# Batched 64x64 matmul: three of the eight a tiles loaded in 8 KB rows by two casting transfers each, with no fp32 quarter

## The chip, the core and the metric

The kernel runs on one core of a Trainium2 chip. That core has five engines with instruction streams of their own: TensorE (PE; its weight loads are shown as PEld), VectorE (DVE), ScalarE (ACT), GpSimd (POOL) and SyncE (SP), and 16 DMA engines that move data between HBM and the on-chip SBUF. Three of the instruction streams issue transfers here, each into a queue of its own: SP into queue q1, ScalarE into q10, GpSimd into q0. Only GpSimd's transfers can convert the data type on the way. The metric is the device time of one execution in microseconds (us).

## What is computed

```python
a: float32 (1024, 64, 64)     b: float32 (1024, 64, 64)
out = np.matmul(a, b)         # 1024 products of 64 x 64 matrices, float32
```

Each input has 16.78 MB, and so has the output. The kernel multiplies in bfloat16 (bf16) and accumulates in fp32.

## The kernel before

**Tiles.** a comes in 8 tiles of 128 batches (`s` = 0 to 7, 2.1 MB each), b and the output in 16 tiles of 64 batches (`t` = 0 to 15, 1.05 MB each). The loop runs over t; tile s of a serves t = 2s and 2s + 1.

**Loading a.** `load_a(s)` cuts a tile into four quarters h (batch = 4g + h). Partition p of a quarter holds 16 consecutive rows of one matrix, 1024 fp32 numbers, 4 KB that are contiguous in HBM. Quarters 0 to 2 are loaded by GpSimd (line 74), which casts to bf16 on the way (`a_sb`); quarter 3 is loaded as fp32 by SP (line 78, `a_raw`) and cast by an engine. Both come from `a_pool` with three buffers each. Tile 0 is loaded in another way (`load_first_a`: four fp32 quarters, two on SP and two on ScalarE). Tiles 1 and 2 are asked for before the loop, 3 and 4 behind tile 1's transposes, tile s + 4 in the iteration t = 2s for s = 1 to 3.

**Loading b.** `load_b(t)` loads a whole tile in one transfer (rows of 512 B, line 97), on SP for even t and on ScalarE for odd t, from three buffers: b(t+3) is issued when b(t) was cast to bf16 (`cast`, line 173, VectorE but for t = 0 and part of 15). Each issuing engine works in order: what is behind a transfer that waits for its buffer waits too.

**Transposing a.** TensorE needs a with k on the partitions. Pairs of bf16 are handled as one fp32 element (bitcast). For tiles 0 and 4 to 7, `regroup` puts the quarters side by side, TensorE transposes them (line 138) and ScalarE copies the result out of PSUM (line 141). For tiles 1, 2 and 3 (`ON_DVE`), VectorE transposes in blocks of 32x32, once for each quarter (line 128), straight from the loaded tile; the fp32 quarter is first cast by ScalarE (line 126) into a buffer of `work`.

**Spreading.** `spread(t)` copies the transposed a into a block-diagonal tile `at_bd` (two buffers, zeroed once): four copies of 32 partitions for the TensorE tiles (line 164), eight for the VectorE tiles (line 154). Then `multiply(t)` runs 64 pairs of weight load and matmul (line 218), ScalarE copies the products out of PSUM (line 206, for late tiles with VectorE), and `store` writes them one iteration later: tiles 0 to 13 by GpSimd (line 195), 14 by SP, 15 by SP and ScalarE.

**Order.** The schedule is written by hand: each engine executes its instructions in the order of the Python program. On VectorE, from t = 0 on: spread(1), cast(1), the four transposes of tile 1, spread(2), cast(2), the four transposes of tile 2, spread(3), cast(3), two transposes of tile 3, spread(4), cast(4), the other two, spread(5), cast(5), and so on. On SP the order is half of tile 0, b0, a_raw of tile 1, b2, a_raw of tiles 2, 3 and 4, b4, a_raw of 5, b6 and so on; on GpSimd the casting loads of tiles 1, 2, 3 and 4, then the store of t = 0, tile 5, and stores and loads in turn.

Of the kernel before, what the change touches and what calls it, by code (L numbers as in the profile page):

```python
# [8 lines left out]
fp32 = mybir.dt.float32  # L9
bf16 = mybir.dt.bfloat16  # L10
# [3 lines left out]
def kernel(  # L14
# [14 lines left out]
    nc = tc.nc  # L29
# [9 lines left out]
    ON_DVE = (1, 2, 3)  # L39

    a_v = a.rearrange("(s g h) (mp v) k -> s h g mp (v k)", h=4, g=32, v=16)
    b_v = b.rearrange("(t g h) (kp u) n -> t (h kp) g (u n)", h=4, g=16, u=2)
    o_v = out.rearrange("(t gh x) (mo w) n -> t (x mo) gh (w n)", gh=8, x=8, w=4)

    consts = ctx.enter_context(tc.tile_pool(name="consts", bufs=1))
    a_pool = ctx.enter_context(tc.tile_pool(name="a_pool", bufs=A_AHEAD))
    b_pool = ctx.enter_context(tc.tile_pool(name="b_pool", bufs=B_AHEAD))
    work = ctx.enter_context(tc.tile_pool(name="work", bufs=2))
# [13 lines left out]
    a_tiles, b_tiles, abf_tiles, at_tiles, bbf_tiles = {}, {}, {}, {}, {}  # L62
# [5 lines left out]
        return nc.scalar if t == n_t - 1 and lo % 4 == 0 else nc.sync  # L68

    def load_a(s):  # L70

        a_sb = a_pool.tile([128, 3, 16, 64], bf16, name="a_sb")
        for h in range(3):
            nc.gpsimd.dma_start(  # L74
                out=a_sb[:, h, :, :].rearrange("p v k -> p (v k)"), in_=a_v[s, h], single_packet=True
            )
        a_raw = a_pool.tile([128, 16, 64], fp32, name="a_raw")
        nc.sync.dma_start(out=a_raw[:].rearrange("p v k -> p (v k)"), in_=a_v[s, 3])
        a_tiles[s] = a_sb, a_raw

    def load_first_a():

# [17 lines left out]
    def regroup(s):  # L100
        a_sb = a_tiles.pop(s)
        a_bf = work.tile([128, 16, 4, 64], bf16, name="a_bf")
        if s == 0:
            for h in range(4):
                copy = nc.scalar.copy if h % 2 else nc.vector.tensor_copy
                copy(a_bf[:, :, h, :], a_sb[h].rearrange("p (v k) -> p v k", v=16))  # L106
        else:
            cast_sb, raw = a_sb
            nc.vector.tensor_copy(  # L109
                a_bf[:, :, 0:3, :], cast_sb[:].rearrange("p h v k -> p v h k")  # L110
            )
            nc.vector.tensor_copy(a_bf[:, :, 3, :], raw[:])  # L112
        abf_tiles[s] = a_bf
        at_tiles[s] = work.tile([128, 32, 4, 4, 4], fp32, name="at_sb")

    def transpose_dve(s, half):
        cast_sb, raw = a_tiles[s]
        if half == 0:
            at_tiles[s] = work.tile([128, 4, 8, 4, 4, 4], fp32, name="at_sb")
        for h in (2 * half, 2 * half + 1):  # L120
            rows = cast_sb[:, h, :, :] if h < 3 else None
            if h == 3:
                rows = work.tile([128, 16, 4, 64], bf16, name="a_bf")[:, 0:4, :, :].rearrange(
                    "p x y k -> p (x y) k"
                )
                nc.scalar.copy(rows, raw[:])  # L126
            pairs = rows.rearrange("p v k -> p (v k)").bitcast(fp32)
            nc.vector.transpose(  # L128
                at_tiles[s][:, h].rearrange("p g w mp vo -> p w vo g mp"),
                pairs.rearrange("p (vo w kp) -> p w vo kp", vo=4, w=4),  # L130
            )

    def transpose(s, j):
        a_cols = abf_tiles[s][:].rearrange("p v h k -> p v (h k)").bitcast(fp32)
# [11 lines left out]
    def spread(t):  # L146
        bd = bd_tiles[t % N_BD]
        at_sb = at_tiles[t // 2]
        for h in range(4):
            rows = slice(32 * h, 32 * h + 32)  # L150
            if t // 2 in ON_DVE:
                for i in range(2):
                    block = 32 * (2 * (t % 2) + i)
                    nc.vector.tensor_copy(  # L154
                        bd[rows, 8 * i : 8 * i + 8, :, h, :, :].rearrange(
                            "p g w mp vo -> p (g w) (mp vo)"
                        ),
                        at_sb[block : block + 32, h].rearrange(
                            "p g w mp vo -> p (g w) (mp vo)"
                        ),  # L160
                    )
            else:
                half = slice(16 * (t % 2), 16 * (t % 2) + 16)
                nc.vector.tensor_copy(  # L164
                    bd[rows, :, :, h, :, :].rearrange("p g w mp vo -> p (g w) (mp vo)"),
                    at_sb[rows, half].rearrange("p g w mp vo -> p (g w) (mp vo)"),
                )
# [71 lines left out]
    with tc.manual_schedule():  # L239
# [7 lines left out]
        make_identity(nc, identity)  # L247
        nc.gpsimd.memset(bd_tiles[1][:, 0:8], 0.0)
        load_a(1)
        load_b(2)  # L250
        nc.gpsimd.memset(bd_tiles[1][:, 8:16], 0.0)
        load_a(2)
        regroup(0)
        transpose(0, 0)
        transpose(0, 1)
        spread(0)
        cast(0)
        for t in range(n_t):
            s, half = t // 2, t % 2
            if t + 1 < n_t:  # L260
                spread(t + 1)
                cast(t + 1)
            if t + B_AHEAD < n_t:
                load_b(t + B_AHEAD)
            if half == 0 and 0 < s < n_s - 1 - A_AHEAD:
                load_a(s + 1 + A_AHEAD)
            if half == 0 and 0 < s < n_s - 1 and s + 1 not in ON_DVE:
                transpose(s + 1, 1)
            multiply(t)
            if t == 0:  # L270
                transpose_dve(1, 0)
                transpose_dve(1, 1)
                a_tiles.pop(1)
                load_a(A_AHEAD)
                load_a(A_AHEAD + 1)
            if t and s + 2 in ON_DVE and (half or s):
                for part in [0, 1] if t == 1 else [half]:
                    transpose_dve(s + 2, part)
                if half:
                    a_tiles.pop(s + 2)  # L280
            elif half == 0 and 0 < s and s + 2 < n_s:
                regroup(s + 2)
            elif half == 1 and s + 2 < n_s:
                transpose(s + 2, 0)
            if t >= HOLD - 1:
                store(t - HOLD + 1)
# [32 lines left out]
```

## Time and profile before

| What | Value |
|---|---|
| Time, median of 3 runs | 133.86 us (133.62 to 133.91) |
| The profiled execution: its time, its span | 133.61 us, 131.8 us |
| Busy: DVE, ACT, PE, POOL | 101.8, 88.1, 59.6, 31.9 us |
| VectorE's transposes, line 128 | 9 of `a_sb`, mean 1065 ns; 3 of `a_bf`, mean 1049 ns |
| ScalarE's casts of the fp32 quarter, line 126 | 3, mean 1046 ns |
| Casting loads of a, line 74 | 21 of 256 KB written (half of what is read), median 15.9 us to landing |
| Plain loads of a quarter, line 78 | 7 of 512 KB, median 17.3 us to landing |
| Copies into the block diagonal, line 154 | 48 of 32x512, mean 457 ns |

The span runs from the first to the last instruction of the profiled execution; the time of an execution has some 1.8 us around it. The busy time of an engine says how long it had work, not that it set the pace: what counts is which wait ends last. A line of the timeline gives the start, the duration and the engine, the line of the kernel, the operation and its output and input, the number of instructions merged, and in brackets how long the engine had been idle and who ended that. In the windows each engine has its busy time and its number of instructions; then come TensorE's granted clock, the busy share of the DMA engines and the GB/s written. In the queue table a casting transfer counts with the bytes that it writes, half of those that it reads.

### The profile page before, as it was taken

The numbers are of one execution on the slowest core, as the hardware profiler recorded it, in microseconds if no ns is written. First come the engines' busy times: TensorE is split into PE (matmuls) and PEld (weight loads), VectorE is DVE, ScalarE is ACT, GpSimd is POOL, SyncE is SP. The second block draws the span as 40 slices with busy tenths as digits, with TensorE's granted clock in tenths as the row PEclk, the third lists the DMA queues.
The fourth block names the chain that finished last, engine by engine and source line by source line (L and its number), as shares of the span: only waits on it lengthen the run. The fifth ranks groups of instructions, "written<-read, shape, count | busy, mean of one in ns | idle before, by whom it ended". The sixth has DMA issues, their size and how long they took to land.

```text
span 131.8 us, 2750 instructions
## 1 busy us (share of the span) xinstructions
PE 59.6 (45%) x1104; PEld 56.7 (43%) x1104; DVE 101.8 (77%) x144; ACT 88.1 (67%) x158; POOL 31.9 (24%) x43
## 2 busy tenths in 40 slices
PE   0006405730550640908662883299369619465000
PEld 0006305730550630908552872298368618464000
DVE  5930399529999984999999998699999997898300
ACT  2125414999495096492999989469969996549920
POOL 8991000340054000618031204300420302040000
PEclk9999975798568555595999599558968975579855
DMA  3999999999999999999999999999999999999993
GB/s 68 372 334 313 306 313 280 280 311 321 327 299 400 362 306 297 393 393 400 321 285 357 403 395 362 308 299 385 395 391 393 390 390 397 399 395 406 390 383 136
DMA packets 19020, 44.99 MB, mean 341 GB/s; under 512 B 1088, under 2 KB 3136, under 8 KB 19008
## 3 DMA queue, kind: packets, MB, share of 16 engines
q0 software_dynamic: 6832, 20.19, 50.6%
q1 hardware_dynamic: 7120, 14.68, 30.7%
q10 hardware_dynamic: 5056, 9.96, 20.1%
q8 instruction: 8, 0.13, 0.4%
q14 instruction: 4, 0.03, 0.1%
HBM read 33.55 MB, written 16.78 MB: 382 GB/s over the span
## 4 chain that ended last, share of the span: by engine, by line
DMA 53%; ACT 15%; DVE 14%; PE 6%; issue 5%; SPq 2%; ACTq 0%; DVEq 0%
DMA b_sb<-in_b_dram 53%; ACT o_sb L206 12%; PE o_ps L218 6%; DVE at_bd L164 4%; DVE b_bf L173 4%; DVE at_bd L154 2%; ACT b_bf L173 1%; DVE at_sb L128 1%; DVE o_sb L206 1%; DVE a_bf L109 1%; SPq L91 1%; ACT a_bf L126 1%; SPq L97 1%; ACT b_bf L180 1%; DVE a_bf L112 0%
## 5 line engine op out<-in xcount | busy, mean ns | idle before, releaser
L206 ACT COPY o_sb<-o_ps 64x512 f32<-64x512 f32 x112 | 65.0, 581 | 17.9 <-PE o_ps L218 13.5
L218 PEld LDWEIGHTS <-at_bd 128*128 128x128 bf16 x1024 | 45.2, 117 | 52.6 <-DVE b_bf L173 40.5
L218 PE MATMUL o_ps<-b_bf,at_bd 128*128 128x64 bf16 x960 | 45.6, 223 | 48.7 <-DVE b_bf L173 35.0
L164 DVE COPY at_bd<-at_sb 32x1024 f32<-32x1024 f32 x40 | 29.6, 739 | 6.6 <-ACT at_sb L141 5.6
L195 POOL DMA_DIRECT2D out_dram<-o_sb x14 | 15.4, 1103 | 46.1 <-ACT at_sb L141 20.6
L154 DVE COPY at_bd<-at_sb 32x512 f32<-32x512 f32 x48 | 22.0, 457 | 1.1
L74 POOL DMA_DIRECT2D a_sb<-in_a_dram x21 | 12.4, 606 | 38.5 <-DVE at_sb L128 33.2
L173 DVE CAST b_bf<-b_sb 128x2048 bf16<-128x2048 f32 x14 | 17.2, 1227 | 5.2 <-DMA b_sb<-in_b_dram 4.9
L138 PE MATMUL at_ps<-identity,a_bf 128*128 128x128 f32 x80 | 12.9, 329 | 11.0 <-ACT a_bf L106 11.0
L138 PEld LDWEIGHTS at_ps<-identity,a_bf 128*128 128x128 f32 x80 | 11.7, 176 | 11.0 <-issue 11.0
L141 ACT COPY at_sb<-at_ps 128x512 f32<-128x512 f32 x20 | 10.8, 591 | 2.7 <-PE at_ps L138 2.0
L128 DVE STREAM_TRANSPOSE at_sb<-a_sb 128x512 f32<-128x512 f32 x9 | 8.9, 1065 | 0.0
L128 DVE STREAM_TRANSPOSE at_sb<-a_bf 128x512 f32<-128x512 f32 x3 | 3.1, 1049 | 4.0 <-ACT a_bf L126 4.0
L206 DVE COPY o_sb<-o_ps 64x512 f32<-64x512 f32 x8 | 5.5, 690 | 0.2
L106 ACT CAST a_bf<-o_sb 128x1024 bf16<-128x1024 f32 x2 | 2.1, 1045 | 5.0 <-DMA o_sb<-in_a_dram 5.0
L173 ACT CAST b_bf<-b_sb 128x2048 bf16<-128x2048 f32 x1 | 1.9, 1897 | 4.0 <-DMA b_sb<-in_b_dram 4.0
L126 ACT CAST a_bf<-a_raw 128x1024 bf16<-128x1024 f32 x3 | 3.1, 1046 | 1.7 <-DMA a_raw<-in_a_dram 1.7
L109 DVE COPY a_bf<-a_sb 128x3072 bf16<-128x3072 bf16 x4 | 4.2, 1045 | 0.0
L106 DVE CAST a_bf<-o_sb 128x1024 bf16<-128x1024 f32 x2 | 2.8, 1383 | 1.8 <-DMA o_sb<-in_a_dram 1.8
L246 DVE MEMSET at_bd<- 128x4096 f32 x1 | 3.5, 3472 | 0.8 <-issue 0.8
L206 DVE COPY o_sb<-at_ps 64x256 f32<-64x256 f32 x8 | 3.4, 422 | 0.5 <-PE at_ps L218 0.4
L180 ACT CAST b_bf<-b_sb 128x512 bf16<-128x512 f32 x2 | 1.1, 616 | 3.5 <-DMA b_sb<-in_b_dram 3.5
(16 smaller groups left out, 15.4 us busy)
## 6 DMA issues: line engine op xcount, KB each, us to landing
out_dram<-o_sb POOLq DMA_DIRECT2D x14, 1024.0 KB, 22.7
a_sb<-in_a_dram POOLq DMA_DIRECT2D x21, 256.0 KB, 15.9
a_raw<-in_a_dram SPq DMA_DIRECT2D x7, 512.0 KB, 17.3
o_sb<-in_a_dram SPq DMA_DIRECT2D x2, 512.0 KB, 5.9
o_sb<-in_a_dram ACTq DMA_DIRECT2D x2, 512.0 KB, 7.0
out_dram<-o_sb SPq DMA_DIRECT2D x2, 512.0 KB, 5.5
out_dram<-o_sb SPq DMA_DIRECT2D x2, 256.0 KB, 5.2
out_dram<-o_sb ACTq DMA_DIRECT2D x2, 256.0 KB, 4.7
```

The costliest lines, as they stand in the source:

```text
L74: nc.gpsimd.dma_start(out=a_sb[:, h, :, :].rearrange("p v k -> p (v k)"), in_=a_v[s, h], single_packet=True)
L106: copy(a_bf[:, :, h, :], a_sb[h].rearrange("p (v k) -> p v k", v=16))
L109: nc.vector.tensor_copy(a_bf[:, :, 0:3, :], cast_sb[:].rearrange("p h v k -> p v h k"))
L128: nc.vector.transpose(at_tiles[s][:, h].rearrange("p g w mp vo -> p w vo g mp"), pairs.rearrange("p (vo w kp) -> p w vo kp", vo=4, w=4),)
L138: nc.tensor.transpose(at_ps[:, vo, :], a_cols[:, 4 * vo + 2 * j + wl, :], identity[:])
L141: nc.scalar.copy(at_tiles[s][:, :, 2 * j + wl, :, :], at_ps[:].rearrange("p vo (g mp) -> p g mp vo", mp=4),)
L154: nc.vector.tensor_copy(bd[rows, 8 * i : 8 * i + 8, :, h, :, :].rearrange("p g w mp vo -> p (g w) (mp vo)"), at_sb[block : block + 32, h]. ...
L164: nc.vector.tensor_copy(bd[rows, :, :, h, :, :].rearrange("p g w mp vo -> p (g w) (mp vo)"), at_sb[rows, half].rearrange("p g w mp vo -> p ...
L173: (nc.vector.tensor_copy if t else nc.scalar.copy)(b_bf[:], b_sb[:])
L195: store_queue(t, lo).dma_start(out=o_v[t, :, lo : lo + n, :], in_=o_sb[:, lo : lo + n].rearrange("p gh j wl n -> p (gh j wl n)"),)
L206: copies[2 * par + wl](dst, src)
L218: nc.tensor.matmul(o_ps[:, gl, g % 2, j, :], at_bd[:, j, g, :, u], b_bf[:, g, 64 * u : 64 * u + 64], start=(u == 0), stop=(u == 1),)
```

## The change

Tiles 1 to 3 are cut into two halves instead of four quarters (batch = 2g + h; partition p holds 32 consecutive rows of one matrix, 2048 fp32 numbers, 8 KB contiguous in HBM). Each half is one casting transfer on GpSimd, and both halves have the same form: there is no fp32 quarter in these tiles, no transfer of one on SP and no cast of it on ScalarE. VectorE transposes a half in one instruction of 1024 fp32 elements for each partition. In the transposed tile, a row of a matrix is now found at (gm, vo) with 4 x 8 in place of (mp, vo) with 4 x 4, where gm holds the parity of g beside the half of the matrix; `spread` picks the 2 x 8 block that belongs to a copy, so that each of its runs is 16 elements of 64 bytes as before, with 128 bytes from one run to the next in the source instead of 64. The other tiles are loaded as before, but from one room for all kinds of tile: `a_sb` and `a_raw` are now parts of one buffer of 10,240 bytes per partition, the same size as the two had together.

In the order of each engine: SP no longer has the a_raw of tiles 1, 2 and 3, so that b2 follows b0, then come a_raw of tile 4, b4, a_raw of 5, b6. GpSimd issues two loads, not three, for each of tiles 1 to 3. VectorE has one transpose where it had two.

```diff
+    a_v8 = a.rearrange("(s g h) (mp v) k -> s h g mp (v k)", h=2, g=64, v=32)
...
     def load_a(s):
-        a_sb = a_pool.tile([128, 3, 16, 64], bf16, name="a_sb")
+        room = a_pool.tile([128, 5120], bf16, name="a_sb")
+        if s in ON_DVE:
+            a_sb = room[:, 0:4096].rearrange("p (h x) -> p h x", h=2)
+            for h in range(2):
+                nc.gpsimd.dma_start(out=a_sb[:, h, :], in_=a_v8[s, h], single_packet=True)
+            a_tiles[s] = a_sb
+            return
+        a_sb = room[:, 0:3072].rearrange("p (h x) -> p h x", h=3)
         for h in range(3):
-            nc.gpsimd.dma_start(
-                out=a_sb[:, h, :, :].rearrange("p v k -> p (v k)"), in_=a_v[s, h], single_packet=True
-            )
-        a_raw = a_pool.tile([128, 16, 64], fp32, name="a_raw")
-        nc.sync.dma_start(out=a_raw[:].rearrange("p v k -> p (v k)"), in_=a_v[s, 3])
-        a_tiles[s] = a_sb, a_raw
+            nc.gpsimd.dma_start(out=a_sb[:, h, :], in_=a_v[s, h], single_packet=True)
+        raw = room[:, 3072:5120].bitcast(fp32)
+        nc.sync.dma_start(out=raw, in_=a_v[s, 3])
+        a_tiles[s] = (
+            a_sb.rearrange("p h (v k) -> p h v k", v=16),
+            raw.rearrange("p (v k) -> p v k", v=16),
+        )
...
-    def transpose_dve(s, half):
-        cast_sb, raw = a_tiles[s]
-        if half == 0:
-            at_tiles[s] = work.tile([128, 4, 8, 4, 4, 4], fp32, name="at_sb")
-        for h in (2 * half, 2 * half + 1):
-            rows = cast_sb[:, h, :, :] if h < 3 else None
-            if h == 3:
-                rows = work.tile([128, 16, 4, 64], bf16, name="a_bf")[:, 0:4, :, :].rearrange(
-                    "p x y k -> p (x y) k"
-                )
-                nc.scalar.copy(rows, raw[:])
-            pairs = rows.rearrange("p v k -> p (v k)").bitcast(fp32)
-            nc.vector.transpose(
-                at_tiles[s][:, h].rearrange("p g w mp vo -> p w vo g mp"),
-                pairs.rearrange("p (vo w kp) -> p w vo kp", vo=4, w=4),
-            )
+    def transpose_dve(s, h):
+        if h == 0:
+            at_tiles[s] = work.tile([128, 2, 8, 4, 4, 8], fp32, name="at_sb")
+        nc.vector.transpose(
+            at_tiles[s][:, h].rearrange("p g w gm vo -> p w vo g gm"),
+            a_tiles[s][:, h, :].bitcast(fp32).rearrange(
+                "p (vo w kp) -> p w vo kp", vo=8, w=4
+            ),
+        )
...
             if t // 2 in ON_DVE:
+                gp = h // 2
...
-                        at_sb[block : block + 32, h].rearrange(
+                        at_sb[block : block + 32, h % 2, :, :, 2 * gp : 2 * gp + 2, :].rearrange(
```

More of the change, by code (lines that the diff above doesn't have):

```diff
@@ L109, in regroup @@
             nc.vector.tensor_copy(
-                a_bf[:, :, 0:3, :], cast_sb[:].rearrange("p h v k -> p v h k")
+                a_bf[:, :, 0:3, :], cast_sb.rearrange("p h v k -> p v h k")
             )
-            nc.vector.tensor_copy(a_bf[:, :, 3, :], raw[:])
+            nc.vector.tensor_copy(a_bf[:, :, 3, :], raw)
         abf_tiles[s] = a_bf
         at_tiles[s] = work.tile([128, 32, 4, 4, 4], fp32, name="at_sb")
-    def transpose_dve(s, half):
-        cast_sb, raw = a_tiles[s]
-        if half == 0:
-            at_tiles[s] = work.tile([128, 4, 8, 4, 4, 4], fp32, name="at_sb")
-        for h in (2 * half, 2 * half + 1):
-            rows = cast_sb[:, h, :, :] if h < 3 else None
-            if h == 3:
-                rows = work.tile([128, 16, 4, 64], bf16, name="a_bf")[:, 0:4, :, :].rearrange(
-                    "p x y k -> p (x y) k"
-                )
-                nc.scalar.copy(rows, raw[:])
-            pairs = rows.rearrange("p v k -> p (v k)").bitcast(fp32)
-            nc.vector.transpose(
-                at_tiles[s][:, h].rearrange("p g w mp vo -> p w vo g mp"),
-                pairs.rearrange("p (vo w kp) -> p w vo kp", vo=4, w=4),
-            )
+    def transpose_dve(s, h):
[7 more added lines that the diff above has]
+        )
     def transpose(s, j):
```

## The prediction

> **What bounds the kernel now.** First the page's slices, its HBM line and the queue table; then the chain that ended last; then the DMA queues cut to short windows; then VectorE's timeline.
>
> The page: busy tenths of the 16 DMA engines in 40 slices, GB/s moved in each, HBM bytes.
> ```profile
> DMA  3999999999999999999999999999999999999993
> ...
> HBM read 33.55 MB, written 16.78 MB: 382 GB/s over the span
> ```
> The transfers fill every slice but the two at the ends. 50.33 MB at 382 GB/s is the span, 131.8 us. What the change could save on an engine is therefore worth only what it does to the transfers, or to the tail after the last load.
>
> The chain that ended last (start us, us, what):
> ```profile
> 2.48 16.73 DMA b_sb<-in_b_dram
> ...
> 29.93 21.27 DMA b_sb<-in_b_dram
> ...
> 51.23 1.23 DVE b_bf L173
> ...
> 102.47 14.73 DMA b_sb<-in_b_dram
> ...
> 125.87 0.37 ACT o_sb L206
> ```
> The chain is made of waits for b loads, and behind the last one (b15, landing at 117.2) of ScalarE's evacuations until 126.2 and the last stores.
>
> The queue table of the window 10 to 18 us (packets, MB written, share): q0 is GpSimd's queue, q1 SP's, q10 ScalarE's.
> ```profile
> q0 software_dynamic: 416, 0.76, 49.9%
> q1 hardware_dynamic: 415, 0.85, 30.7%
> q10 hardware_dynamic: 417, 0.85, 27.4%
> ```
> Here q0 carries casting a rows (4 KB read, 2 KB written), q1 and q10 carry b in packets of 2 KB. The three queues take turns packet by packet, 416 : 415 : 417. In bytes read q0 therefore has a half and b0 and b1 a quarter each (0.85 MB in 8 us is 106 GB/s). Whoever has larger packets has more of the bandwidth: this carries the prediction.
>
> VectorE's timeline:
> ```profile
> 20.93 1.23 DVE L173 CAST b_bf<-b_sb 128x2048 bf16<-128x2048 f32 x1
> 22.07 2.87 DVE L128 STREAM_TRANSPOSE at_sb<-a_sb 128x512 f32<-128x512 f32 x3
> 28.93 1.06 DVE L128 STREAM_TRANSPOSE at_sb<-a_bf 128x512 f32<-128x512 f32 x1 [3.99 <-ACT a_bf L126]
> 29.84 3.44 DVE L154 COPY at_bd<-at_sb 32x512 f32<-32x512 f32 x8
> 33.30 1.23 DVE L173 CAST b_bf<-b_sb 128x2048 bf16<-128x2048 f32 x1
> ...
> 45.68 3.50 DVE L154 COPY at_bd<-at_sb 32x512 f32<-32x512 f32 x8
> 51.23 1.23 DVE L173 CAST b_bf<-b_sb 128x2048 bf16<-128x2048 f32 x1 [2.04 <-DMA b_sb<-in_b_dram]
> ```
> VectorE loses 3.99 us to ScalarE's cast of the fp32 quarter, then makes up the time and waits 2.04 us for b4 all the same.
>
> The tail, in windows (the last number is GB/s):
> ```profile
> 126.00:128.00 2.00, 0.00 (x0) 0.00 (x0) 0.00 (x0) 0.24 (x1) 0.00 (x0) 0.50 1.08 382
> 128.00:130.00 2.00, 0.00 (x0) 0.00 (x0) 0.00 (x0) 0.00 (x0) 0.00 (x0) 0.50 0.86 301
> 130.00:132.00 2.00, 0.00 (x0) 0.00 (x0) 0.00 (x0) 0.00 (x0) 0.00 (x0) 0.50 0.08 26
> ```
> From 126 us on 1.42 MB move (2 x 0.382 + 2 x 0.301 + 2 x 0.026), the last packet near 130.6. At the 401 GB/s of the window 116 to 120 (q0 alone) they need 3.54 us, not 4.6. So an earlier end of the evacuations can win at most 1.05 us; beyond that the bytes decide.
>
> **The change part by part.** All sums stand against the profiled execution's 133.61 us (span 131.8), which is 0.25 us under the median 133.86.
>
> *Transfers.* Bytes in HBM stay. For tiles 1 to 3, 1,152 cast packets of 4 KB and 384 plain ones of 4 KB become 768 of 8 KB (source sides). Packet records (medians): cast 172 ns, plain 4 KB 159 to 172, b's 2 KB 84. Two of 84 are 168, so a packet's fixed part lies between nothing and 9 ns: 768 x 9 / 16 engines = 0.43 us gained at most. If the fp32 quarters at 159 ns become cast bytes at 172: 384 x 13 / 16 = 0.31 us lost. Between these I take 0, as the plain quarter's median is 172 too.
>
> *Issue.* POOL issues 18 a transfers, not 21 (mean 606 ns, 1.8 us less); SP loses three issues, and ScalarE three casts of 1.05 us. None of these engines sets the end in that stage, so 0. On SP, b2 and b4 are no longer queued behind a_raw 1 to 3 (1.57 MB); a_raw of tile 4 now waits for the second transpose of tile 1, with b4 behind it.
>
> *VectorE.* Twelve transposes of 512 columns become six of 1024. Three took 2.87 us, 0.957 each; two of these are 1.91 us, less at most one fixed part (the 128x1 memset takes 59 ns): 1.85. Twice the longest single one, 1.085, is 2.17. I take 1.87, as pitch and not duration adds up. Wider target strides (32 B for 16) have no row. The 48 spread copies (L154, median 419 ns) now read 64-byte runs; their target already has such runs, so 0; the slow end is the PSUM copies' 690 ns for 512 columns, 13 us in all.
>
> *The start, by turns.* q0's first packet comes at 7.1 us. With 8 KB packets q0's share against 2 KB packets is 2/3, 268 of 402 GB/s, and b0 and b1 have 67 each.
> - The rest of a0 ends at 8.6 (q1) and 10.1 (q10), half a us to 1 us later; q0 has 0.65 MB by then and b0 0.09.
> - b0: 0.96 MB at 67 GB/s, 24.5 us (before: 18.9). b1: 1.05 MB, 25.8 (19.7).
> - a1 to a3, 6.29 MB: 4.84 by 25.8, then 4/5 of 402 beside b2 alone: 30.3 (32.9).
> - VectorE: cast(1) 26.2 to 27.4, two transposes to 31.1 (before 29.9), so spread(2) to 34.5; b2 lands near 32.5, so no wait: cast(2) 34.5, 1.2 us later than before.
> - a4 and b4 are issued at 31.1 (a4's casts before: 25.2). Until their first packet there is left 0.6 MB of b2 and b3's 1.05 MB (issued 26.8 behind ScalarE's cast): 1.65 MB, 4.1 us from 30.3, to 34.4. Issue to first packet took 1.4 us at the start (0.74 to 2.16) and 4.4 for b3 (21.2 to 25.6): 32.5 to 35.5. So the DMA engines stand idle for 0 to 1.1 us. I take 0.7, nearer the loaded case.
> - Then q1 has a_raw 4 alone ahead of b4: 0.52 MB at 200 GB/s and 1.05 at 133, later 100: b4 near 47 (50.8). VectorE gets there through cast(2) 34.5, transposes 39.5, spread(3) 43, cast(3) 44.2, transpose 46.1, spread(4): cast(4) at 49.6, 1.6 us earlier than 51.23.
> - ScalarE's issue of b7 waits for this cast (52.5, now 50.9), and from b7 on q10 goes on from load to load to b15. So b15 can land up to 1.6 us earlier.
>
> *Sum.* Tail: 1.6, capped by the bytes at 1.05 us gained. DMA idle near 32 us: 0.7 lost. Price of packets 0. Net -0.35: 133.26, with 0.25 to the median 133.5.
>
> Two rules of the Trainium skill speak against the change. "DMA: Bandwidth & Descriptors" (section SWDGE vs HWDGE vs iDMA) wants a packet of GpSimd's queue to be at most 4096 B; q0 shows none above that before, in 10 to 18 us 172 ns each. If the rows are cut to it, the shares stay as they are and the sum would be the -1.05 us of the second rival. "SBUF — State Buffer" (section SBUF: two separate sides) says that VectorE's two-port copies lock GpSimd out from writing descriptors, while SP's transfers are immune; the first cast's packet at 7.14, 4.1 us behind its issue at 3.00 and just as VectorE's cast of 2.07 us ended, agrees. By it a4 would begin behind spread(2)'s copies, at about 34.5 to 35.5, idle 1.1 us, and the sum would be +0.05: 133.9.
>
> **The rivals.**
> 1. *The DMA engines run dry (slower).* Place: 30 to 36 us, between a3's landing and a4's first packet. For it: b0, the start of all compute, lands 5.6 us later, and a4 is issued 5.9 us later. Against: b2 and b3 bridge 4.1 us. Price: 1.1 us of idle by the long latency, and no lead carried to the tail: 133.61 + 1.1 + 0.25 = 135.0. It decides from 1.05 us of idle on, that is if a4's first packet comes after 35.4; each us that the transposes take beyond 1.87 x 2 adds as much.
> 2. *The rows are cut into 4 KB packets.* Shares as before, b0 at 18.9; no 3.99 us wait, spread(2) at 25.8 and not 29.8, a4 not late, no idle. The tail's cap alone: -1.05, 132.8. For it: no larger packet is in the trace; against: a plain row of 4 KB is one packet, and so is a cast one.
> 3. *Hidden anyway.* b15's landing is set by q10's share beside the stores, and the lead only makes VectorE wait (as the 2.04 us did): 133.9.
> 4. *The spread copies lose their rate.* VectorE has some 2 us of slack until 51 us, so it begins at 2 / 48 = 42 ns each; at 690 ns it costs 11 us, 145. Against: the L164 copies, 739 ns for 1024 columns, have the same rate as L154.
>
> **How the numbers follow.** The runs before lie within 0.2% of their median, so 0.27 us is about what can be told from no change. Chances: forecast 0.38 (133.5, own range 132.9 to 134.0), rival 1 0.28, rival 2 0.14, rival 3 0.14, rival 4 0.06. Faster: 0.38 x 0.75 + 0.14 x 0.95 + 0.14 x 0.2 = 0.45. Slower: 0.28 x 0.9 + 0.06 x 0.95 + some 0.02 each of the forecast and rival 3 = 0.35. Same: 0.20. Range: below, 1.05 and 0.43 off the median, 132.4; above, rival 1 with 0.2 us of dearer packets or transposes, 135.2. Rival 4's far end and a little on either side stay outside.
>
> **What would show it.** Right: packets of 4096 B written on q0 before 31 us, twice as long as the 172 ns; q0 : q1 : q10 still equal in packets but b0's cast on ScalarE starting near 24.9, not 19.2; a short hole in the DMA slices near 31 to 35 us; VectorE's wait for b4 gone and its cast(4) before 51.2; the last evacuation before 126.2. Wrong: b0 at 19 (rival 2), transposes much over 1.9 us or copies L154 over 460 ns (rivals 1 and 4), a hole over 1 us (rival 1), b15 landing at 117 in spite of a lead (rival 3).

## The result, and the profile after

The changed kernel takes 135.31 us (median of 5, 135.08 to 135.44) against 133.86 us for the kernel before on the same chip (median of 5, 133.57 to 133.99). The ratio is 1.0113, with a 95% interval of 1.0098 to 1.0129: slower by 1.1%. The profiled execution took 135.31 us with a span of 133.5 us; the one of before took 133.61 us with 131.8 us. So 1.7 us have to be found.

The page of the changed kernel: busy tenths of the DMA engines, the groups of the spread copies and of VectorE's transposes (busy us, mean ns of one, idle before), HBM bytes.

```profile
DMA  3999999999999999999999999999999999999992
...
HBM read 33.55 MB, written 16.78 MB: 377 GB/s over the span
...
L156 DVE COPY at_bd<-at_sb 32x512 f32<-32x512 f32 x48 | 21.8, 454 | 1.1
...
L127 DVE STREAM_TRANSPOSE at_sb<-a_sb 128x1024 f32<-128x1024 f32 x6 | 11.5, 1966 | 0.0
```

The same bytes at 377 GB/s instead of 382. There is no hole in the DMA slices, none that would show in tenths. The transposes and the copies cost what was expected.

The queue table of the changed kernel from 10 to 18 us (packets, MB written, share):

```profile
q0 software_dynamic: 294, 1.07, 66.1%
q1 hardware_dynamic: 289, 0.59, 21.4%
q10 hardware_dynamic: 290, 0.58, 18.6%
```

The packets of the three queues are still equal in number, but q0's are now written in 4 KB (8 KB read). So b0 and b1 come later, as VectorE's timeline shows (start, duration, work, in brackets the wait before it):

```profile
25.18 1.23 DVE L175 CAST b_bf<-b_sb 128x2048 bf16<-128x2048 f32 x1 [3.35 <-DMA b_sb<-in_b_dram]
26.32 3.80 DVE L127 STREAM_TRANSPOSE at_sb<-a_sb 128x1024 f32<-128x1024 f32 x2
29.98 3.64 DVE L156 COPY at_bd<-at_sb 32x512 f32<-32x512 f32 x8
34.22 1.23 DVE L175 CAST b_bf<-b_sb 128x2048 bf16<-128x2048 f32 x1 [0.60 <-DMA b_sb<-in_b_dram]
...
50.13 1.23 DVE L175 CAST b_bf<-b_sb 128x2048 bf16<-128x2048 f32 x1
```

cast(1) is at 25.18 (before: 20.93), cast(4) at 50.13 without a wait (before: 51.23 with one of 2.04). The compute has overtaken the kernel before by 1.1 us there, and keeps that to the end. The chain that ended last (start us, us, what) shows it at b15:

```profile
3.67 30.46 DMA b_sb<-in_b_dram
34.22 1.23 DVE b_bf L175
...
100.68 15.04 DMA b_sb<-in_b_dram
```

The last long wait ends at 115.72, before at 117.20. Compute ended earlier, and the kernel still became slower. So the loss must be in the transfers. The queue tables from 30 to 36 us, of the kernel before and then of the changed one:

```profile
q1 hardware_dynamic: 259, 0.97, 42.6%
q0 software_dynamic: 256, 0.46, 40.7%
q10 hardware_dynamic: 259, 0.53, 23.2%
```

```profile
q10 hardware_dynamic: 527, 1.05, 61.8%
q1 hardware_dynamic: 291, 0.70, 35.9%
q0 software_dynamic: 45, 0.08, 7.2%
```

GpSimd's queue is all but empty in these 6 us, because a3 has landed (30.5 us, from the packet records) and a4 has only just been asked for. GpSimd's timeline shows the request, for which GpSimd had waited 21.71 us, until the transposes of tile 1 were done (before: at 25.23):

```profile
30.42 1.63 POOL L81 DMA_DIRECT2D a_sb<-in_a_dram  x3 [21.71 <-DVE at_sb L127]
```

But the engines are not idle. The windows of the changed kernel (busy us and number of instructions of PE, PEld, DVE, ACT, POOL; clock; DMA share; GB/s written):

```profile
30.00:32.00 2.00, 1.10 (x32) 1.00 (x32) 1.95 (x6) 1.95 (x4) 1.58 (x3) 1.00 1.04 327
32.00:34.00 2.00, 1.30 (x25) 1.30 (x25) 1.55 (x4) 1.94 (x5) 1.10 (x2) 0.62 1.06 291
34.00:36.00 2.00, 1.07 (x21) 0.91 (x19) 1.78 (x2) 1.95 (x5) 0.10 (x1) 0.50 1.08 304
```

A share of 1.04 to 1.08 says busy throughout, yet only 291 to 327 GB/s arrive, and what arrives here is nearly all plain, so that written is also read. Reckoned in bytes read, with q0's counted twice, the changed kernel has 1.05 + 0.70 + 0.16 = 1.91 MB in these 6 us, 318 GB/s, and the kernel before 0.97 + 0.92 + 0.53 = 2.42 MB, 403 GB/s. A packet of b3 takes 118 ns here (median); before, and beside larger packets, one of b takes 84 to 96.

**A ledger of the transfers.** To put prices on places, I added up the bytes read of all packets (casting packets by what they read) in stretches of the span, and took from each stretch's length what these bytes would need at 400 GB/s. The result is us lost against 400 GB/s; below zero, the stretch ran faster.

| Stretch, us | before | after | difference |
|---|---|---|---|
| 0 to 8 | 2.98 | 3.03 | +0.05 |
| 8 to 30 | -0.10 | -0.67 | -0.57 |
| 30 to 36 | -0.08 | 1.22 | +1.30 |
| 36 to 124 | 0.44 | 0.50 | +0.06 |
| 124 to the last landing | 1.08 | 1.45 | +0.37 |
| last landing | 130.58 | 131.76 | +1.18 |
| from there to the end of the span | 1.24 | 1.76 | +0.52 |

The stretches add up to 1.21 us (the last landing is 1.18 us later), and with the 0.52 us behind it they are the 1.7 us: 1.3 lost in the stretch 30 to 36 us, 0.57 won before it by the larger packets, 0.37 lost in the tail, and 0.5 behind the last landing. Most of the last is, by the records of the instructions, GpSimd's clearing of the semaphores at the end: it began 0.35 us behind TensorE's drain in the changed kernel (133.06 and 132.71 us) and together with it before (131.37 and 131.38).

The tail of the changed kernel in windows (columns as above):

```profile
124.00:126.00 2.00, 0.00 (x0) 0.00 (x0) 0.00 (x0) 0.73 (x2) 0.00 (x0) 0.66 1.03 370
126.00:128.00 2.00, 0.00 (x0) 0.00 (x0) 0.00 (x0) 0.00 (x0) 0.00 (x0) 0.50 1.05 359
128.00:130.00 2.00, 0.00 (x0) 0.00 (x0) 0.00 (x0) 0.00 (x0) 0.00 (x0) 0.50 1.04 348
130.00:132.00 2.00, 0.00 (x0) 0.00 (x0) 0.00 (x0) 0.00 (x0) 0.00 (x0) 0.50 0.50 172
```

ScalarE has finished by 125 us (before: 126.2), but 2.5 MB are still to be stored (2 x 370 + 2 x 359 + 2 x 348 + 2 x 172, in KB/us). GpSimd's stores, which came late with everything else in the queues, land at 126.9 (before: 125.2, both by packet records). What was won on the engines found the DMA engines still full.

### The profile page after: what moved, and what is told of

Same layout as the page of the kernel before. It is cut to its first block, busy times and chain, and to the rows that moved or that the text cites. A ratio compares the mean times of both kernels' runs of the same rounds, so it can differ in the third digit from the quotient of the medians.

```text
span 133.5 us, 2737 instructions
## 1 busy us (share of the span) xinstructions
PE 62.5 (47%) x1104; PEld 59.4 (44%) x1104; DVE 101.2 (76%) x138; ACT 84.9 (64%) x155; POOL 32.6 (24%) x40
## 4 chain that ended last, share of the span: by engine, by line
DMA 46%; DVE 28%; ACT 9%; issue 6%; SPq 2%; PE 1%; DVEq 0%; ACTq 0%
DMA b_sb<-in_b_dram 46%; ACT o_sb L208 9%; DVE at_bd L156 8%; DVE at_bd L166 6%; DVE at_sb L127 6%; DVE b_bf L175 5%; PE o_ps L220 1%; DVE a_bf L120 1%; SPq L105 1%; DVE o_sb L208 1%; SPq L99 1%; DVE a_bf L117 1%; ACT b_bf L182 1%; ACT at_sb L142 0%; DVEq L208 0%
## 5 line engine op out<-in xcount | busy, mean ns | idle before, releaser
L220 PEld LDWEIGHTS <-at_bd 128*128 128x128 bf16 x1024 | 47.4, 119 | 49.1 <-DVE b_bf L175 33.5
L220 PE MATMUL o_ps<-b_bf,at_bd 128*128 128x64 bf16 x960 | 46.4, 224 | 45.1 <-DVE b_bf L175 31.5
L197 POOL DMA_DIRECT2D out_dram<-o_sb x14 | 16.6, 1189 | 38.6 <-ACT at_sb L142 15.3
L139 PEld LDWEIGHTS at_ps<-identity,a_bf 128*128 128x128 f32 x80 | 12.2, 182 | 12.0 <-issue 12.0
L127 DVE STREAM_TRANSPOSE at_sb<-a_sb 128x1024 f32<-128x1024 f32 x6 | 11.5, 1966 | 0.0
L114 DVE CAST a_bf<-o_sb 128x1024 bf16<-128x1024 f32 x2 | 2.2, 1098 | 2.6 <-DMA o_sb<-in_a_dram 2.5
L220 PE MATMUL at_ps<-b_bf,at_bd 128*128 128x64 bf16 x64 | 3.6, 241 | 0.9 <-ACT b_bf L182 0.9
```

Source lines behind the costliest of these rows:

```text
L127: nc.vector.transpose(at_tiles[s][:, h].rearrange("p g w gm vo -> p w vo g gm"), a_tiles[s][:, h, :].bitcast(fp32).rearrange("p (vo w kp) ...
L139: nc.tensor.transpose(at_ps[:, vo, :], a_cols[:, 4 * vo + 2 * j + wl, :], identity[:])
L197: store_queue(t, lo).dma_start(out=o_v[t, :, lo : lo + n, :], in_=o_sb[:, lo : lo + n].rearrange("p gh j wl n -> p (gh j wl n)"),)
L220: nc.tensor.matmul(o_ps[:, gl, g % 2, j, :], at_bd[:, j, g, :, u], b_bf[:, g, 64 * u : 64 * u + 64], start=(u == 0), stop=(u == 1),)
```

## The experiments

Four theories were set against each other.

1. *The gap alone*: the stretch at 30 to 36 us costs the time, by the low rate of b's packets alone.
2. *The late start of compute*: b0 and b1 land 5 us later, and this is what costs.
3. *The burden on GpSimd's queue*: three more quarters go through casting transfers of GpSimd.
4. *Three places*, formed after the first runs: the gap, a stall at 8 to 12 us in some variants, and the tail, each costing what its rate says.

In the diffs, `s in (...)` lists the tiles that are loaded in rows of 8 KB; the others of tiles 1 to 3 get two transfers for each half, with rows of 4 KB. All ratios are to the kernel before on the same chip, with a 95% interval.

### Rows of 4 KB in all three tiles

```diff
             for h in range(2):
-                nc.gpsimd.dma_start(out=a_sb[:, h, :], in_=a_v8[s, h], single_packet=True)
+                runs = [slice(0, 2048)] if s in () else [slice(0, 1024), slice(1024, 2048)]
+                for r in runs:
+                    nc.gpsimd.dma_start(out=a_sb[:, h, r], in_=a_v8[s, h][:, :, r], single_packet=True)
```

> The changed kernel with one thing undone: each half of tiles 1 to 3 is loaded by two casting transfers of 4 KB rows, not by one of 8 KB rows. No fp32 quarter, the large transposes and the queues stay as changed. Theory 1 (the gap: 8 KB packets double GpSimd's share, b0 and b1 come 5 us late, a4 is asked for late, and between a3's landing and a4's first packet only b's packets are left, which move at 290 GB/s where 400 are usual): b0 lands near 19 us, no window of 30 to 36 us under 390 GB/s read, time 133.0 to 133.9. Theory 2 (late start: compute begins 5 us late and this is never made up): the same here, 133.0 to 133.9. Theory 3 (burden: three quarters more on GpSimd's queue push its stores back into the tail): stays at 135.3.

Measured: 134.96 against 133.58 us, 1.0104 (1.0089 to 1.0118). The gap at 30 to 36 us is gone (ledger -0.01 us), b0 is cast at 20.4 us (before: 19.2, changed: 24.1), and the kernel is nearly as slow as the changed one. Theories 1 and 2 missed the time. The ledger shows two other places: 0.54 us lost at 8 to 12 us, and 1.75 us behind 124 us. The first one in windows, of the kernel before and then of this one:

```profile
9.00:10.00 1.00, 0.00 (x0) 0.00 (x0) 0.66 (x1) 0.14 (x1) 0.78 (x1) 1.00 1.10 301
```

```profile
9.00:10.00 1.00, 0.00 (x0) 0.00 (x0) 0.69 (x1) 0.00 (x0) 1.00 (x2) 1.00 0.96 211
```

In this us the rate falls from 301 to 211 GB/s written with the engines 0.96 busy; a casting packet takes 222 ns there on average instead of 172, one of SP's b 118 instead of 96. The medians stay at 172 and 96, so it is some packets that take much longer. Theory 3 hit the time; the run with quarters below shows that its reason was wrong.

### 8 KB rows in tiles 1 and 2 only

```diff
-                runs = [slice(0, 2048)] if s in () else [slice(0, 1024), slice(1024, 2048)]
+                runs = [slice(0, 2048)] if s in (1, 2) else [slice(0, 1024), slice(1024, 2048)]
```

> 8 KB rows for tiles 1 and 2, 4 KB rows (two transfers for each half) for tile 3. b0 and b1 should still land near 24 and 25 us, but tile 3 lasts until about 33 us, so that the gap is filled. Theory 1 (gap): most of the loss is gone, 133.6 to 134.2. Theory 2 (late start): stays at 135.3. Theory 3 (burden): stays at 135.3.

Measured: 134.46 us, 1.0066 (1.0051 to 1.0081). b0 is as late as in the changed kernel (24 us), and tile 3 keeps GpSimd's queue going longer. Its queue table from 30 to 36 us:

```profile
q10 hardware_dynamic: 524, 1.04, 54.4%
q0 software_dynamic: 190, 0.35, 31.2%
q1 hardware_dynamic: 139, 0.43, 21.0%
```

With 190 packets of q0 in the place of 45, the stretch loses 0.54 us, not 1.22, and the ratio is 0.5% below the changed kernel's. As b0 is just as late, this speaks against theory 2, and as the load on GpSimd's queue is the same, against theory 3. Theory 1 missed too, by 0.3 us: the gap is only half filled, and 1.46 us are lost behind 124 us.

### 8 KB rows in tile 3 only

```diff
-                runs = [slice(0, 2048)] if s in () else [slice(0, 1024), slice(1024, 2048)]
+                runs = [slice(0, 2048)] if s in (3,) else [slice(0, 1024), slice(1024, 2048)]
```

> 8 KB rows for tile 3 alone, 4 KB rows for tiles 1 and 2. b0 lands near 19 us, and the 8 KB packets come when b0 and b1 have landed. Theories 1 and 2: no gap, no late start, 133.0 to 133.8. Theory 3 (burden): 135.3.

Measured: 134.96 us, 1.0099 (1.0081 to 1.0118). No gap (-0.14 us), but the stall at 8 to 12 us again (0.65 us) and 1.92 us behind 124. Theories 1 and 2 missed once more. What the runs with the stall share is tile 1 in rows of 4 KB, each of them one half of 8 KB.

### The rates by themselves

A kernel that leaves out the product and only moves data: each stage starts when the one before has landed. The lines are shortened.

```diff
+        for t in range(6):                       # A: b alone, SP and ScalarE
+            load_b(t)
+        nc.gpsimd.dma_start(out=a4[i][:, 1024 * h : 1024 * h + 1024], in_=a_v[i, h], single_packet=True)       # B
+        nc.gpsimd.dma_start(out=a8[i][:, 2048 * h : 2048 * h + 2048], in_=a_v8[2 + i, h], single_packet=True)  # C
...                                              # D: as C beside b; E: 4 KB rows, no cast; F, G: stores
```

> No matmul: the kernel only moves data, in stages that wait for one another, and leaves the product out. Stage A: six b tiles on SP's and ScalarE's queues alone. B: casts of 4 KB rows alone. C: casts of 8 KB rows alone. D: casts of 8 KB rows beside b. E: plain 4 KB rows on two queues. F: stores by GpSimd. G: stores by SP and ScalarE. Theory 1 (gap): A runs near 290 GB/s, B near 400, C near 410 to 420 (source bytes), D near 410, so that it is the lack of other packets beside b's that costs. Theories 2 and 3: A near 400 as everything else, and the low rate at 30 to 36 us was a lack of requests.

Measured, in windows inside the stages (busy DVE, ACT, POOL; clock; DMA share; GB/s written). In order: A b alone; B casts of 4 KB; C casts of 8 KB; D casts of 8 KB beside b, and in the row behind it the rest of b alone, when the casts have landed; E plain 4 KB rows; F stores of GpSimd; G stores of SP and ScalarE.

```profile
6.00:22.00 16.00, 2.32 (x32) 0.41 (x1) 0.00 (x0) 1.00 1.06 290
30.00:36.00 6.00, 1.78 (x20) 0.00 (x0) 0.22 (x1) 1.00 1.12 206
46.00:51.00 5.00, 1.16 (x16) 0.00 (x0) 0.00 (x0) 1.00 1.06 213
59.00:69.00 10.00, 0.95 (x12) 0.00 (x0) 0.00 (x0) 1.00 1.06 280
71.00:75.00 4.00, 0.94 (x12) 0.00 (x0) 0.00 (x0) 1.00 1.06 292
82.00:85.00 3.00, 0.67 (x8) 0.00 (x0) 0.00 (x0) 1.00 1.02 416
90.00:96.00 6.00, 0.15 (x1) 0.00 (x0) 0.93 (x2) 1.00 1.00 312
105.00:112.00 7.00, 0.00 (x0) 0.00 (x0) 0.00 (x0) 1.00 1.04 344
```

b alone moves 290 GB/s with the DMA engines 1.06 busy; the casts read 412 (4 KB) and 426 GB/s (8 KB), twice what they write; plain rows of 4 KB move 416, and the two mixed read some 414 (the casts' 1.34 MB written count twice, beside 0.73 MB in each of b's queues, in 10 us). When the casts are through, b falls to 292 at once. So the low rate of the gap is b's own rate when nothing larger runs beside it, without any compute: (2.4 - 6 x 0.290) / 0.4 = 1.65 us would be lost if the 6 us of the gap held b alone; with the few q0 packets and a_raw of tile 4 in it, 1.22 us were. The stores need care: F moves 312 GB/s here, where GpSimd's stores in the kernel before moved 401 (116 to 120 us), and why is open; so the 344 of G is a rate of this kernel and not a limit.

### 8 KB rows in tiles 1 and 3

```diff
-                runs = [slice(0, 2048)] if s in () else [slice(0, 1024), slice(1024, 2048)]
+                runs = [slice(0, 2048)] if s in (1, 3) else [slice(0, 1024), slice(1024, 2048)]
```

> 8 KB rows for tiles 1 and 3, 4 KB rows (two transfers for each half) for tile 2. The rates of the runs so far, against 400 GB/s, put the loss of the changed kernel into a gap at 30 to 36 us (1.2 us), of the 4 KB variant into a stall at 8 to 12 us (0.5 us) and of all variants into the tail behind 124 us (0.4 to 0.8 us more than before). Here the start has two issues ahead of the memset as in the changed kernel, b0 lands near 21 us and a4 is asked for while tile 3 still moves. Theory 4 (three places: gap, stall and tail each cost what the rates say): no gap, no stall, 0.2 to 0.3 us gained by 8 KB packets, 0.4 us lost in the tail: ratio 1.000 to 1.004. Theory 1 (the gap alone): 0.996 to 0.999. Theory 3 (burden of three more quarters on GpSimd's queue, wherever): 1.008 to 1.012.

Measured: 133.91 against 133.71 us, 1.0014 (1.0002 to 1.0026). No gap (-0.10), no stall (-0.13): tile 1 in rows of 8 KB avoids the stall, and tile 2 in rows of 4 KB, which are read later, brings none (-0.26 us from 12 to 30 us). This is theory 4's number.

### The store of t = 14 by GpSimd, in that variant and in the kernel before

```diff
-        if t < n_t - 2:
+        if t < n_t - 1:
             return nc.gpsimd
```

> As the one before, and in addition the store of t = 14 is issued by GpSimd, not by SP, so that it goes out in 4 KB packets behind GpSimd's other stores and not in 1 KB packets beside them. Theory 4 (tail: the earlier end of compute puts SP's 1 KB packets beside GpSimd's stores, at 360 to 375 GB/s): 0.3 to 0.6 us faster than the one before, ratio 0.994 to 1.000. Theory 3: no change from the one before.

> The kernel before with the store of t = 14 issued by GpSimd and nothing else. Theory 4: the kernel before has little of this mixing (GpSimd's stores end at 125.0 us), so it gains less than the variant does: 0 to 0.3 us, ratio 0.997 to 1.001. Theory 3: the same gain or loss as in the variant.

Measured: the variant with tiles 1 and 3 becomes slower by it, 134.37 us, 1.0046 (1.0032 to 1.0061), and loses 1.58 us behind 124 us where it had lost 1.34. The kernel before stays as it is: 133.85 us, 1.0007 (0.9995 to 1.0020). Theory 4 had expected a gain in the variant. The edit did not end the mixing of packets of 1 KB and 4 KB, though: the stores of t = 15 still go out in 1 KB, and GpSimd's now last until 130.05 us beside them in the variant (125.85 without the edit) and until 129.53 in the kernel before (125.20). In the kernel before, these some 4 us more of mixing cost 0.04 us of the tail (1.12 for 1.08). So mixing by itself does not explain the long tail, and what does stays open.

### Rows of 4 KB, with the second memset earlier

Before the fourth casting transfer of tile 1, GpSimd does a memset that else stands behind it, so that GpSimd's transfers are issued with the same break as before the change.

```diff
+                    if s == 1 and h == 1 and r.start:
+                        nc.gpsimd.memset(bd_tiles[1][:, 8:16], 0.0)
...
-        nc.gpsimd.memset(bd_tiles[1][:, 8:16], 0.0)
```

> The 4 KB variant of the first series with GpSimd's second memset moved from behind the fourth transfer of tile 1 to behind the third, where it stood before the change. Theory 4 (the stall at 8 to 12 us comes from four issues ahead of that memset): the stall is gone, 0.5 us faster than the 4 KB variant, ratio 1.004 to 1.007, with the tail's loss left. If the stall is of another origin: 1.009 to 1.012.

Measured: 134.82 us, 1.0084 (1.0064 to 1.0104), between the two ranges, with 0.80 us lost at 8 to 12 us in the profiled execution. The stall does not come from four transfers being issued ahead of the memset.

### Four buffers for a, and two controls

If tile 4 has a buffer of its own, its load need not wait for the transposes of tile 1. The room is taken from two of the eight output buffers, and two controls show what that alone does: fewer output buffers in the changed kernel, and both edits in the kernel before.

```diff
-    a_pool = ctx.enter_context(tc.tile_pool(name="a_pool", bufs=A_AHEAD))
+    a_pool = ctx.enter_context(tc.tile_pool(name="a_pool", bufs=A_AHEAD + 1))
...
-    o_pool = ctx.enter_context(tc.tile_pool(name="o_pool", bufs=8))
+    o_pool = ctx.enter_context(tc.tile_pool(name="o_pool", bufs=6))
```

> The changed kernel with four buffers for a tiles, not three (and six for output tiles, not eight, to make room): tile 4 needs no buffer of tile 1, so its transfers are asked for at the start, behind tile 3's, and not after tile 1's transposes. Packets, queues and the late b0 and b1 stay as changed. Theory 4 (the gap at 30 to 36 us costs 1.2 us because a4 is asked for too late): no window there under 390 GB/s read, ratio 0.998 to 1.004. Rival (the late start of compute costs, gap or not): 1.009 to 1.013.

> Control for the one before: the changed kernel with six buffers for output tiles, not eight, and three for a as it has. If six are enough the ratio is that of the changed kernel, 1.010 to 1.013; what it is above that, the run before pays too.

> Second control: the kernel before with four buffers for a and six for output tiles. It has no gap at 30 to 36 us, so theory 4 gives no gain: ratio 0.998 to 1.003. If it gains as much as the changed kernel does from the fourth buffer (1 percent), the buffer helps for another reason than the gap.

Measured: the changed kernel with four buffers 133.76 against 133.72 us, 1.0012 (0.9999 to 1.0024); with fewer output buffers alone 135.31 us, 1.0117 (1.0098 to 1.0135); the kernel before with both 133.76 us, 1.0002 (0.9991 to 1.0014). So the fourth buffer takes 1.05% off the changed kernel and nothing off the kernel before. The queue table of the changed kernel with four buffers from 30 to 36 us, and its cast of b1 in VectorE's timeline:

```profile
q0 software_dynamic: 306, 0.56, 49.1%
q1 hardware_dynamic: 310, 0.77, 35.8%
q10 hardware_dynamic: 244, 0.50, 21.7%
```

```profile
25.27 1.23 DVE L175 CAST b_bf<-b_sb 128x2048 bf16<-128x2048 f32 x1 [3.30 <-DMA b_sb<-in_b_dram]
```

GpSimd's queue is full through the stretch, which now loses -0.02 us in the place of 1.22, while b1 is cast as late as in the changed kernel (25.18). Theory 2 is refuted by that. What moved is the request for tile 4 (its casts from 30.42 to 8.39 us, SP's quarter from 30.15 to 10.80) and, with it, what stands behind it in the queues (b4 from 31.17 to 26.59, tile 5 from 39.40 to 34.38). By the ledger 1.24 us are won from 30 to 36 us, and the profiled span is 1.26 us shorter: the gap is shown to be the cause of the larger part. The rest of this variant's ledger: 0.6 us won by the 8 KB packets at 8 to 30 us, 0.5 us lost in the tail, and 1.78 us from the last landing to the end of the span (before: 1.24).

### The fourth quarter cast by GpSimd as well, in the kernel before

Tiles 1 to 3 keep their quarters of contiguous 4 KB rows, but all four are casting transfers; no fp32 quarter, no cast of it, twelve small transposes.

```diff
-        for h in range(3):
+        for h in range(4 if wide else 3):
...
-            rows = cast_sb[:, h, :, :] if h < 3 else None
-            if h == 3:
...
+            rows = cast_sb[:, h, :, :]
```

> The kernel before with one part of the change alone: no fp32 quarter in tiles 1 to 3. The fourth quarter is a casting transfer of GpSimd like the others, in contiguous rows of 4 KB, and VectorE transposes it straight from the tile; layout and the twelve small transposes stay as before. In the 4 KB variants of the change a stall at 8 to 12 us cost 0.5 to 0.8 us; they read 4 KB out of each 8 KB. If the stall comes from that reading: none here, ratio 1.001 to 1.005. If it comes from four and more issues of casts early on: it is here too, ratio 1.007 to 1.011.

Measured: 133.96 against 133.72 us, 1.0015 (1.0004 to 1.0026), no stall (-0.03 us at 8 to 12) and a tail of 1.06 us as before. So the three quarters more on GpSimd's queue cost 0.2 us: theory 3 is refuted. And since this kernel also reads 4 KB rows at the start without a stall, the stall most likely belongs to the way the other variants read them, 4 KB out of every 8 KB, at the start. Its mechanism was not tested.

None of the versions beats the kernel before: five of them (four buffers in the changed kernel and in the kernel before, tiles 1 and 3, the store of t = 14 in the kernel before, quarters) are within 0.2% of it.

## Why the prediction was wrong

It said 133.5 us, with a range of 132.4 to 135.2 us; it was 135.31 us. Two steps failed. The bridge between a3 and a4 was taken to leave 0.7 us of idle time and cost 1.30 us by a low rate; the tail was taken to win 1.05 us and lost 0.37. Against the forecast's own sum (-0.35 us; measured +1.7) the bridge is 0.6 us of the miss and the tail 1.42. The cause of the first is shown, that of the second only in part.

**Right.** The turns packet by packet (294 : 289 : 290), and with them b0 (24.06 us, predicted 24.5), cast(1) (25.18, predicted 26.2), a3's landing (30.5, predicted 30.3), the request for a4 (30.42, predicted 31.1) and its first packet (35.3, in the predicted 32.5 to 35.5). The transposes (3.80 us for two, predicted 3.74) and the copies (454 ns, 457 before). The end of the wait for b4, and the lead on the engines: cast(4) 1.1 us earlier (predicted 1.6), the last long wait 1.5 us earlier. So rivals 2 and 4 are out; the third was right that the lead wins nothing, but not on the reason: b15 did land earlier.

**Wrong: "left is 1.65 MB, 4.1 us from 30.3", idle 0 to 1.1 us, taken as 0.7.** This is a bridge at some 400 GB/s, by b2 and b3 alone. But b alone moves 290 GB/s, so the bridge lasted longer and there was no idle time at all: the loss of 1.22 us is in the rate. The 84 ns of a b packet was taken beside q0's larger packets and carried over to a stretch where these are missing; there it is 118 ns. Rival 1 had the place right and the mechanism wrong: the engines did not run dry, they ran slow, and a4's first packet (35.3) came just before the 35.4 that it named as its condition. That its price of 135.0 came near is luck: its 1.1 us of idle time stand in the place of a slow stretch, a gain by packets and a longer tail.

**Wrong: the tail wins 1.05 us.** The step set the last 1.42 MB at the 401 GB/s of a stretch in which GpSimd's queue ran alone. But the last bytes are stores of SP and ScalarE in packets of 1 KB: from 126 to 128 us they moved 382 GB/s in the kernel before, the tail of the changed kernel ran at 348 to 370, and by themselves such stores moved 344 in the kernel of the rates. At 344 GB/s the 1.42 MB need 4.13 us, and the cap would have been 0.45 us. Besides, the DMA engines were not ahead but 0.84 us behind at 124 us (the ledger's sum up to there). Neither is the whole reason. With four buffers the DMA engines were 0.54 us ahead at 124 us (the same sum for that run) and ScalarE's last copies 0.92 us ahead, as these lines show, of the kernel before and then of the one with four buffers:

```profile
125.11 1.12 ACT L206 COPY o_sb<-at_ps 64x256 f32<-64x256 f32 x3
```

```profile
124.19 1.13 ACT L208 COPY o_sb<-at_ps 64x256 f32<-64x256 f32 x3
```

The last packet landed there at 130.48 us, against 130.58 before: 0.10 us of a lead of 0.9 reached the end. So this step would have failed without the gap as well.

**Mis-sized: the price of packets, taken as 0 with at most 0.43 us gained.** A cast of 8 KB took 322 ns, and two of 4 KB take 344: 22 ns saved, more than the 9 ns that were worked out from b's packets. On 16 engines 22 ns for each of the 768 packets are 1.06 us; the stretch from 8 to 30 us won 0.57.

**Not thought of: 0.5 us behind the last landing.**

With the measured terms in the prediction's own sum: 1.30 lost in the gap, 0.57 won by packets, 0.37 lost in the tail, 0.52 behind it and 0.1 in small differences make 133.61 + 1.7 = 135.3.

Of the two rules that were weighed, the first, that a packet of GpSimd's queue should preferably have at most 4096 B (the Trainium skill, "DMA: Bandwidth & Descriptors", section SWDGE vs HWDGE vs iDMA), did not decide: packets of 8 KB read and 4 KB written were taken as they were, and cost 6% less per byte (322 for 344 ns). What cost was their share in the turns, and the same page names the turns by whole packets (section Queues, rings and completion order), which the 294 : 289 : 290 agree with. Its table of specifications puts the least transfer for the full rate at 512 B; b's rows of 512 B moved 290 GB/s where rows of 4 KB moved 416, and the measurement decides. The second rule, that VectorE's two-port copies lock GpSimd out from writing descriptors ("SBUF — State Buffer", section SBUF: two separate sides), would fit a4's first packet at 35.3 us, 4.9 us behind its request and behind the spread copies that run from 29.98 to 33.62 us. But a transfer in which GpSimd has no part took nearly as long: ScalarE's b3 was asked for at 26.05 us, with nothing else in its queue, and had its first packet at 30.09, 4.0 us later. No run here took the copies away, so the rule isn't shown.

**Open.** Why the tail is longer in the changed kernel and all its variants (1.34 to 1.92 us lost behind 124 us, against 1.08 before). An earlier end of compute is not enough to explain it: with the quarters the last copy ended at 124.5 us, before at 126.2, and the tail lost 1.06. Why reading 4 KB out of every 8 KB at the start stalls the transfers. What delays GpSimd's clearing of the semaphores.

## What to carry to other kernels

When a queue of large packets is emptied sooner, ask what runs alone behind it, and price that stretch by the rate of those transfers alone, not by their rate beside others: a busy share of 1 says nothing of it. Where the DMA engines bound the kernel, count a lead on the compute engines as nothing until the bytes are ahead as well; with four buffers even both together brought the last landing only 0.10 us forward. And where larger loads free their buffers later, look first at who is waiting for that buffer; here one more buffer for the next tile removed the loss, and the change was then worth nothing either way.

## What the runs showed of the hardware that was not expected

- b's transfers (rows of 512 B, packets of 2 KB) move 290 GB/s alone with a DMA share of 1.06; beside casts of 8 KB the sum read is about 414 GB/s.
- Casting packets of 8 KB take equal turns with packets of 2 KB (294 : 289 : 290), and are cheaper per byte than two of 4 KB (322 against 344 ns).
- Reading 4 KB out of every 8 KB cost 0.5 to 0.8 us at 8 to 12 us, at the start of tile 1, and nothing later: with rows of 4 KB in all three tiles the reading goes on in the same way from 12 to 30 us, at a loss of -0.01 us.
- Stores of SP and ScalarE alone, in packets of 1 KB, moved 344 GB/s in the kernel of the rates, where rows of 4 KB are read at 416.
